# Projecting a query block of one branch ahead of its values, and a shorter stretch of dense work before the first scores

## The chip, the cores and the metric

The kernel runs on one core of one Trainium2 chip. The metric is the device time of one execution in microseconds, as the median of several runs. The engines are named as the profile names them: PE is TensorE's matmuls and PEld its weight loads, DVE is VectorE, ACT is ScalarE, POOL is GpSimd, SP is SyncE, whose queue issues most of the DMAs.

## What is computed

Two layers over one sequence of 1024 tokens of width 1024, float32. Each layer, cut to what matters here:

```python
h = rms_norm(x, g_pre)
p = h @ w_in                      # one projection, split by columns:
(u_a, v_a, gate_a, q_b, k_b, v_b, gate_b, q_c, k_c, v_c, gate_c, merge_logits) = split(p)
y_a = chunk_gmlp(u_a, v_a, ...) * silu(gate_a)
qh, kh = rope(q_b), rope(k_b)     # 8 query heads of 64, 2 key/value heads
y_b = sliding_window_attention(qh, kh, v_b, sinks) * silu(gate_b)   # window 128, softmax with sinks
y_c = stick_breaking_attention(q_c, k_c, v_c) * silu(gate_c)        # 4 heads of 128, causal
gates = sigmoid(merge_logits + b_merge)
merged = gates[0]*(y_a @ w_ba) + gates[1]*(y_b @ w_bb) + gates[2]*(y_c @ w_bc)
x = x + rms_norm(merged @ w_out, g_post)
```

Branch B is the sliding-window attention. The change lies in the order of its projections.

## The kernel before, in words

Every float32 product is made of three matmuls in a rounded format: each operand is split into a high part (a ScalarE cast, L111) and a low part (a VectorE subtraction, L112), and `mm3` (L128 to L130) adds high times high, high times low and low times high. A dense group of the projections is one such triple on 512 columns.

TensorE's instructions stand in the order in which the program issues them. The other engines' orders are set by the Tile scheduler, with its own priorities; they can be read from the built program alone.

The projections of a layer are jobs in one queue, `stream`. A job (`proj_t`) makes 128 output columns for all 1024 tokens: two halves of 512 tokens, each of eight groups accumulated in a PSUM buffer `pj` (two buffers), and an evacuation after each half. `step()` issues one group; `fill(us)` issues groups until a planned time is used up, at 0.64 planned us per group of `proj_t` and 0.32 per group of `proj_n`; `need(label)` issues groups until the named job has ended, and since the end is only noticed when the next step is asked for, it issues the first group of the following job as well. A job loads the weights of the job behind it when it starts.

`queue_layer` sets the jobs' order: values, queries and keys of branch C, then for branch B the first query block `qb(0)`, the keys `kb`, the values `vb`, the other query blocks `qb(1)` to `qb(3)` and the gates, and the values of branch A (`proj_n`). Each `qb(hp)` holds two heads. Its second evacuation (L279) calls `after_q`: `rope` swaps halves of the heads by four DMAs (L292, SP's queue), VectorE multiplies and adds (L293, L294, L295), and for each of two heads ScalarE copies a high part (L346) and VectorE subtracts a low one (L347). `after_k` does alike for the keys (L307, L309). `after_v` sets two deferred steps, 4 and 6 planned us behind `vb`: each transposes half of the values (L323, TensorE) and splits them; the second also makes differences (L330).

`branch_c` goes first and uses up the queue by `fill` between its own matmuls. `branch_b` follows: `need("vb")`, a `fill`, then eight score blocks. `scores(v)` (matmuls L492) needs query block `v // 2`; it uses two `pz` buffers in turn, which ScalarE (L499, L500, L505) and VectorE (L503, L506, a mask) empty, and is followed by a softmax (L510 to L518). scores(0) and scores(1) stand ahead of the loop, scores(v + 2) in its turn v, then `transp` (L526) and `attend` (L550, evacuated by L560 and L561) of block v, with a `fill` between any two.

`dense` comes behind branch B. It first issues what is left of the queue, and then the products of a two-by-two matrix scheme with seven products each. Their weight operands are `wop`; their data operands are the halves of h and the combinations T1, T2, T4 (own tiles) and T3 (written over a part of h once the queue no longer reads it), built on VectorE from blocks of h that are loaded again (L688; L699, L703, L705, L710, then splits). In each scheme the first two products read h, the third T2, the fourth T3. L823 adds products.

## Time and profile before

| what | us |
|---|---|
| median of 3 runs (2031.05 to 2033.9) | 2031.58 |
| the profiled execution | 2034.41 |
| its span, first to last instruction | 2032.7 |
| TensorE busy in the span | 1997.0 |
| VectorE, ScalarE, GpSimd busy | 1250.1, 811.9, 466.5 |

The profile shows one execution. Busy time counts the time in which an engine works on an instruction. An "idle before" with a releaser says how long an engine stood still ahead of an instruction and whose result it took to go on. Two matmuls overlap, the start of one with the end of the one before, so the rate is read from start to start. In the timeline, neighbouring instructions of one kind are merged into a row with a count. Layer 0 takes about the first half of the span, and its branch B starts near 267 us; the same place of layer 1 is near 1270 us.

### The profile page before, as it was taken

Reading aid. Unit: us, or ns where it says so; the run is one execution under the profiler, and the core shown is the slowest. Engines: PE = TensorE matmul, PEld = TensorE weight load, DVE = VectorE, ACT = ScalarE, POOL = GpSimd, SP = SyncE. Lnnn points to the kernel's source line nnn. Section 1 sums busy time; section 2 is a strip of 40 time slices with the busy share of each in tenths; the row PEclk is TensorE's granted clock in tenths of the full one; section 3 lists DMA queues with packets and bytes.
Section 4 is the critical chain, followed back from the end, with each engine's and each line's share of the span. In section 5 each row is a group of like instructions: output and inputs, shape, how many; then the busy total and the mean of one; then the engine's idle time right before and its main releaser. Section 6 shows DMA issues by size and latency. Waiting matters only on the chain.

```text
span 2032.7 us, 26630 instructions
## 1 busy us (share of the span) xinstructions
PE 1997.0 (98%) x10169; PEld 1676.4 (82%) x10169; DVE 1250.1 (62%) x1649; ACT 811.9 (40%) x1485; POOL 466.5 (23%) x489
## 2 busy tenths in 40 slices
PE   7999999999999999999999999999999999999998
PEld 7898878998888888888898988789888888888886
DVE  5465767776767655554545567677866766555533
ACT  6344555532334433213444345554322444332221
POOL 0221301233422220251002222022343322203400
PEclk9999999999999999999999999999999999999999
DMA  7111222233755527732431112233428554376213
GB/s 230 51 39 45 73 73 94 94 104 104 249 198 186 185 93 252 251 116 86 137 125 40 42 53 62 63 104 104 125 99 273 184 194 157 108 269 217 83 52 135
DMA packets 167008, 261.81 MB, mean 129 GB/s; under 512 B 8617, under 2 KB 120289, under 8 KB 166881
## 3 DMA queue, kind: packets, MB, share of 16 engines
q1 hardware_dynamic: 159968, 234.95, 35.7%
q10 hardware_dynamic: 6912, 25.17, 3.0%
q8 instruction: 80, 1.31, 0.3%
q14 instruction: 48, 0.39, 0.1%
HBM read 175.15 MB, written 79.69 MB: 125 GB/s over the span
## 4 chain that ended last, share of the span: by engine, by line
PE 93%; DVE 3%; ACT 2%; issue 1%; DMA 1%; POOL 0%; SPq 0%; DVEq 0%; ACTq 0%; POOLq 0%
PE pj L129 17%; PE pj L128 17%; PE pj L130 16%; PE pz L129 6%; PE pz L128 6%; PE pz L130 6%; PE ptr L128 5%; PE ptr L129 5%; PE ptr L130 5%; PE pav L427 3%; PE pz L492 1%; PE ptr L414 1%; PE pav L550 1%; PE ptr L526 1%; DMA s<-hT 1%
## 5 line engine op out<-in xcount | busy, mean ns | idle before, releaser
L128 PE MATMUL pj<-h,whi 128*128 128x512 f32 x636 | 260.4, 409 | 1.0 <-ACT s L257 0.8
L129 PE MATMUL pj<-h,whi 128*128 128x512 f32 x636 | 252.4, 397 | 0.0
L130 PE MATMUL pj<-h,wlo 128*128 128x512 f32 x636 | 252.0, 396 | 0.0
L111 ACT CAST wop<-s 128x512 fp32r<-128x512 f32 x144 | 88.2, 618 | 172.7 <-PE ptr L130 56.7
L128 PE MATMUL pj<-whi,h 128*128 128x256 f32 x512 | 148.6, 290 | 1.2 <-ACT h L111 1.2
L130 PE MATMUL pj<-whi,h 128*128 128x256 f32 x512 | 144.6, 282 | 1.7 <-DVE h L112 1.7
L112 DVE TENSOR_TENSOR wlo<-wr,whi 128x1024 fp32r<-128x1024 f32 x76 | 103.7, 1366 | 66.0 <-ACT whi L111 65.8
L129 PE MATMUL pj<-wlo,h 128*128 128x256 f32 x512 | 144.1, 281 | 0.0
L130 PEld LDWEIGHTS pj<-h,wlo 128*128 128x128 f32 x636 | 120.0, 189 | 28.7
L128 PEld LDWEIGHTS pj<-h,whi 128*128 128x128 f32 x636 | 120.5, 190 | 24.4 <-ACT s L257 1.7
L129 PEld LDWEIGHTS pj<-h,whi 128*128 128x128 f32 x636 | 120.4, 189 | 20.2
L111 ACT CAST whi<-wr 128x1024 fp32r<-128x1024 f32 x76 | 79.9, 1051 | 136.1 <-PE pj L129 76.9
L948 POOL TENSOR_TENSOR s<-s,s 128x512 f32<-128x512 f32 x56 | 83.1, 1487 | 221.6 <-DVE s L942 200.7
L112 DVE TENSOR_TENSOR wop<-s,wop 128x512 fp32r<-128x512 f32 x144 | 119.3, 833 | 17.4 <-ACT wop L111 17.3
L112 DVE TENSOR_TENSOR wop<-wr,wop 128x512 fp32r<-128x512 f32 x108 | 96.2, 892 | 39.0 <-ACT wop L111 38.9
L397 DVE TENSOR_TENSOR_SCAN s<-s,ones 128x128 f32<-128x128 f32 (+3 forms) x64 | 88.0, 1375 | 49.6 <-POOL s L392 49.4
L111 ACT CAST wop<-wr 128x512 fp32r<-128x512 f32 x108 | 66.2, 618 | 115.4 <-PE ptr L130 30.4
L112 DVE TENSOR_TENSOR s<-ptr,s 128x512 fp32r<-128x512 f32 (+2 forms) x132 | 76.4, 588 | 56.8 <-ACT s L111 56.5
L129 PE MATMUL pj<-h,s 128*128 128x512 f32 x256 | 102.0, 398 | 0.0
L128 PE MATMUL pj<-h,s 128*128 128x512 f32 x256 | 101.1, 395 | 0.0
L130 PE MATMUL pj<-h,s 128*128 128x512 f32 x256 | 100.6, 393 | 0.0
L130 PEld LDWEIGHTS pj<-whi,h 128*128 128x128 f32 x512 | 97.3, 190 | 2.6 <-DVE h L112 2.6
(226 smaller groups left out, 5132.8 us busy)
## 6 DMA issues: line engine op xcount, KB each, us to landing
wr<-in_w_in_dram SPq DMA_DIRECT2D x88, 512.0 KB, 4.1
sg<-s ACTq DMA_DIRECT2D x48, 512.0 KB, 5.2
s<-sg SPq DMA_DIRECT2D x48, 512.0 KB, 5.0
s<-in_w_in_dram SPq DMA_DIRECT2D x36, 512.0 KB, 4.8
s<-in_x_dram SPq DMA_DIRECT2D x16, 512.0 KB, 4.1
hT<-s SPq DMA_DIRECT2D x16, 512.0 KB, 3.2
s<-hT SPq DMA_DIRECT2D x16, 512.0 KB, 3.8
wor<-in_w_out_dram SPq DMA_DIRECT2D x16, 512.0 KB, 3.7
```

What stands on the lines that cost most here:

```text
L111: nc.scalar.copy(hi, raw)
L112: nc.vector.tensor_tensor(lo, raw, hi.bitcast(F32), op=ALU.subtract)
L128: nc.tensor.matmul(acc, lh, rh, start=first, stop=False)
L129: nc.tensor.matmul(acc, lh, rl, start=False, stop=False)
L130: nc.tensor.matmul(acc, ll, rh, start=False, stop=last)
L397: nc.vector.tensor_tensor_scan(t1[:, :kl][:, ::-1], t1[:, :kl][:, ::-1], ones.to_broadcast([P, kl]), 1.0, op0=ALU.mult, op1=ALU.mult)
L414: nc.tensor.transpose(pt[:, b - b0], t2[:, b * P:(b + 1) * P], ident)
L427: nc.tensor.matmul(av, S["v", hd // 2, b // 4][e][:, vs], at4(at, b, f)[:, b % 4], start=ps_ == 0 and b == 0, stop=ps_ == 2 and b == nb - 1)
L492: nc.tensor.matmul(z[:, e * 2 + j], qT[e][:, n * P:(n + 1) * P], kk[i][:, k0:k0 + 256], start=i == 0, stop=i == 1)
L526: nc.tensor.transpose(pt[:, j * P:(j + 1) * P], s[:, (q * 4 + j) * P:(q * 4 + j + 1) * P], ident)
L550: nc.tensor.matmul(av[:, j], w, t.rearrange("p (e j) k -> p e j k", j=2)[:, :, j], start=i == 0, stop=i == len(ops) - 1)
L948: eng.tensor_tensor(acc[dm][:, ts], acc[dm][:, ts], sg[:, ts], op=ALU.add)
```

## The change

Two edits. In the queue, `qb(1)` is put between `kb` and `vb`. In `branch_b`, the first `fill` goes from 8 to 3 planned us.

```diff
         qb(0)
         raw("kb", O_KB, 1.0, after_k)
+        qb(1)
         raw("vb", O_VB, 1.0, after_v)
-        for i in range(1, 4):
-            qb(i)
+        qb(2); qb(3)
...
         need("vb")
-        fill(8)
+        fill(3)
         ready = {0: scores(0)}
         fill(5)
         ready[1] = scores(1)
```

The work is the same. Up to the end of branch C TensorE issues the same number of groups, and `vb`, which had just ended there, is now the job that `need("vb")` still issues whole.

Three places show what the order becomes. The first is VectorE around the two L347 of qb(1), in layer 0. Before, they stand behind the softmax of scores(0) and scores(1) (tiles s_2688 and s_2779) and directly ahead of the mask of scores(2) (L503, s_2869).

```order
L518 TENSOR_TENSOR s_2688<-s_2688,ls 128x1024
L293 TENSOR_TENSOR s_2654<-s_2654,s_2210 128x1024
L294 TENSOR_TENSOR s_2740<-s_2740,s_2211 128x1024
L516 TENSOR_TENSOR ls<-ls,es 128x8
L295 TENSOR_TENSOR s_2654<-s_2654,s_2740 128x1024
L517 RECIPROCAL ls<-ls 128x8
L112 TENSOR_TENSOR wlo<-wr,whi 128x1024
L518 TENSOR_TENSOR s_2779<-s_2779,ls 128x1024
L347 TENSOR_TENSOR s_2748<-s_2654,s_2748 64x1024
L347 TENSOR_TENSOR s_2749<-s_2654,s_2749 64x1024
L503 COPY_PREDICATED s_2869<-mprev,pz 128x2x128
```

In the change, the same engine has them (s_2591 and s_2592) right behind the keys' L309, ahead of the split of the first half of the values (L112 from ptr) and of the mask of scores(0) (L503, s_2721).

```order
L309 TENSOR_TENSOR s_2450<-s_2339,s_2449 64x1024 x2
L112 TENSOR_TENSOR wlo<-wr,whi 128x1024
L293 TENSOR_TENSOR s_2535<-s_2535,s_2210 128x1024
L294 TENSOR_TENSOR s_2583<-s_2583,s_2211 128x1024
L295 TENSOR_TENSOR s_2535<-s_2535,s_2583 128x1024
L347 TENSOR_TENSOR s_2591<-s_2535,s_2591 64x1024
L347 TENSOR_TENSOR s_2592<-s_2535,s_2592 64x1024
L112 TENSOR_TENSOR wlo<-wr,whi 128x1024
L112 TENSOR_TENSOR s_2683<-ptr,s_2683 128x8x64
L503 COPY_PREDICATED s_2721<-mprev,pz 128x2x128
```

The rotation of qb(1) has moved from behind two softmaxes to ahead of the first.

The second place is ScalarE at the end of branch C (L430 is the evacuation of its last attention) in the change: the high copies of qb(1) (L346) stand on either side of the second evacuation of vb (L279 into s_2655), and the value cast (L111 from ptr) and the copies of scores(0) (L499, L500) behind them.

```order
L111 CAST whi<-wr 128x1024
L430 COPY s_2228<-pav 128x256
L279 ACTIVATE s_2655<-pj 128x512
L346 CAST s_2591<-s_2535 64x1024
L279 ACTIVATE s_2655<-pj 128x512
L346 CAST s_2592<-s_2535 64x1024
L111 CAST whi<-wr 128x1024
L111 CAST s_2683<-ptr 128x8x64
L499 COPY s_2721<-pz 128x2x128
```

Before, the value casts follow directly on L430:

```order
L111 CAST whi<-wr 128x1024
L430 COPY s_2228<-pav 128x256
L111 CAST s_2583<-ptr 128x8x64
L326 COPY s_2587<-ptr 128x512
L279 ACTIVATE s_2654<-pj 128x512
```

So the values' evacuation and casts come later against branch C, and the queries' copies are in between.

The third place is VectorE behind the last attention of branch B (its L561 write s_3902 before), where T2 (s_4262), T3 (h_75, in two parts), T4 (s_4269) and the next weight operands are split. Before:

```order
L703 TENSOR_TENSOR s_3927<-s_4257,s_3927 128x1024
L354 COPY s_3893<-pj 128x2x256
L561 TENSOR_TENSOR s_3902<-pav,s_4231 64x256
L705 TENSOR_TENSOR s_4257<-s_4257,s_3929 128x1024
L561 TENSOR_TENSOR s_3902<-pav,s_4231 64x256
L710 TENSOR_TENSOR s_4265<-s_4265,s_4257 128x1024
L112 TENSOR_TENSOR s_4262<-s_4257,s_4261 128x1024
L112 TENSOR_TENSOR h_75<-s_3903,h_74 128x1024
L354 COPY s_4004<-pj 128x2x256
L112 TENSOR_TENSOR wop<-wr,wop 128x512
L112 TENSOR_TENSOR wop<-s_4247,wop 128x512
L112 TENSOR_TENSOR s_4269<-s_4265,s_4268 128x1024
```

In the change (T2 is s_4303, T4 s_4310, and L561 write s_3941):

```order
L561 TENSOR_TENSOR s_3941<-pav,s_4272 64x256
L112 TENSOR_TENSOR wop<-wr,wop 128x512
L354 COPY s_3978<-pj 128x2x256
L112 TENSOR_TENSOR wop<-s_4288,wop 128x512
L705 TENSOR_TENSOR s_4298<-s_4298,s_3968 128x1024
L112 TENSOR_TENSOR h_75<-s_3942,h_74 128x1024
L710 TENSOR_TENSOR s_4306<-s_4306,s_4298 128x1024
L112 TENSOR_TENSOR s_4303<-s_4298,s_4302 128x1024
L823 TENSOR_TENSOR s_4338<-s_4338,pz 128x512
L112 TENSOR_TENSOR s_4310<-s_4306,s_4309 128x1024
L112 TENSOR_TENSOR h_75<-s_3966,h_74 128x1024
```

The first part of T3 and the weight operands have moved ahead, and the second part of T3 now stands behind the addition L823 of the second product. Between the last attention and the first product of `dense`, TensorE has 54 matmuls of the queue before and 15 in the change, in both layers.

## The prediction

> **What bounds the kernel now.** I read the page first: the busy shares and the chain that ended last.

> ```profile
> span 2032.7 us, 26630 instructions
> PE 1997.0 (98%) x10169; PEld 1676.4 (82%) x10169; DVE 1250.1 (62%) x1649; ACT 811.9 (40%) x1485; POOL 466.5 (23%) x489
> PE 93%; DVE 3%; ACT 2%; issue 1%; DMA 1%; POOL 0%; SPq 0%; DVEq 0%; ACTq 0%; POOLq 0%
> ```

> TensorE is busy 98% of the span, and the chain is TensorE for 93%. The diff adds and removes no matmul, so it can only act on the 35.7 us (2032.7 less 1997.0) in which TensorE is not busy, and on matmuls that run slower than they need to. Hence the second view, whom TensorE waited for (us in total, times, longest).

> ```profile
> PE pz L492 <- DVE s L347: 10.1, 4, 4.7
> PE pz L236 <- DVE s L227: 9.2, 2, 8.3
> PE pav L427 <- DVE s L112: 3.0, 2, 1.5
> PE ptr L526 <- DVE s L561: 2.1, 4, 0.9
> ...
> PE pj L128 <- ACT s L257: 0.8, 2, 0.4
> ```

> The largest wait is branch B's scores (L492) waiting for the rotated query copies (L347): 10.1 us in four waits, two in each layer. L236 is the start of the kernel, which the diff does not touch. The third view is TensorE's timeline at that wait, first in layer 0, then the same place in layer 1 (start, duration, in brackets the idle time and its releaser).

> ```profile
> 285.19 2.08 PE L492 MATMUL pz<-s,s 128*128 128x256 f32 x16
> 287.11 0.39 PE L128 MATMUL pj<-h,whi 128*128 128x512 f32 x1
> ...
> 293.87 0.40 PE L130 MATMUL pj<-h,wlo 128*128 128x512 f32 x1
> 298.92 0.77 PE L492 MATMUL pz<-s,s 128*128 128x256 f32 x2 [4.66 <-DVE s L347]
> 300.08 3.36 PE L492 MATMUL pz<-s,s 128*128 128x256 f32 x14 [0.40 <-DVE s L347]
> 303.24 0.63 PE L128 MATMUL pj<-h,whi 128*128 128x512 f32 x1
> ...
> 308.36 0.60 PE L526 MATMUL ptr<-ident,s 128*128 128x128 f32 x4
> ```

> ```profile
> 1288.35 2.08 PE L492 MATMUL pz<-s,s 128*128 128x256 f32 x16
> 1302.07 0.77 PE L492 MATMUL pz<-s,s 128*128 128x256 f32 x2 [4.65 <-DVE s L347]
> 1311.67 0.60 PE L526 MATMUL ptr<-ident,s 128*128 128x128 f32 x4
> ```

> The wait costs more than 5 us a layer, because after it the matmuls are slow: 0.63 us each where they took 0.39. The stretches of time say why (the figure behind POOL is the granted TensorE clock).

> ```profile
> 299.00:303.00 4.00, 3.60 (x15) 3.31 (x16) 1.47 (x2) 0.65 (x2) 0.41 (x1) 0.50 0.52 146
> 305.40:312.00 6.60, 6.60 (x34) 5.41 (x33) 6.25 (x8) 2.60 (x4) 1.27 (x2) 1.00 0.01 1
> ```

> The clock is at 0.50 behind the gap, and at 1.00 from 305.4 on.

> **The stall, sized without a theory of the clock.** Between 287.11 and 293.87 stand 29 matmul starts after the first, so a 128x512 matmul takes 0.233 us and a dense group of three 0.70 us. Sixteen score matmuls take 287.11 - 285.19 = 1.92 us. From the start of scores(1) to the first transpose (L526) the program has scores(1), ten groups, scores(2) and six groups: 1.92 + 6.99 + 1.92 + 4.20 = 15.03 us. Measured: 308.36 - 285.19 = 23.17 in layer 0 and 1311.67 - 1288.35 = 23.32 in layer 1. The stall costs 8.14 and 8.29 us, together 16.4 us; about 5.2 us of each is idle time, 2.9 us the half clock.

> [...]

> **Why the second projection was late, and where it goes.** Before, qb(1) stands behind vb. Its last evacuation, and VectorE's rotation, are these rows (ScalarE first).

> ```profile
> 295.02 0.59 ACT L279 ACTIVATE s<-pj 128x512 f32<-128x512 f32 x1
> ```

> ```profile
> 291.57 1.22 DVE L293 TENSOR_TENSOR s<-s,s 128x1024 f32<-128x1024 f32 x1
> ...
> 296.31 1.22 DVE L518 TENSOR_TENSOR s<-s,ls 128x1024 f32<-128x1024 f32 x1
> 297.56 2.47 DVE L347 TENSOR_TENSOR s<-s,s 64x1024 fp32r<-64x1024 f32 x2
> ```

> The first score block of qb(1), scores(2), stands right there on TensorE; L347 stands behind the softmax of scores(0) and scores(1). In the change qb(1) takes vb's place, which ended just before the last attention of branch C. What surrounded that place:

> ```profile
> 265.27 0.60 ACT L279 ACTIVATE s<-pj 128x512 f32<-128x512 f32 x1
> ```

> ```profile
> 264.52 3.71 DVE L309 TENSOR_TENSOR s<-s,s 64x1024 fp32r<-64x1024 f32 x3
> ...
> 268.26 1.23 DVE L112 TENSOR_TENSOR wlo<-wr,whi 128x1024 fp32r<-128x1024 f32 x1
> ```

> ```profile
> 247.53 2.75 SPq L292 DMA_DIRECT2D s<-s  x4
> ```

> ```profile
> 267.01 0.39 PE L128 MATMUL pj<-h,whi 128*128 128x512 f32 x1
> ```

> So qb(1) is evacuated at 265.9. Its four swap DMAs (moved with it past two weight loads and branch C's output on SP's queue) take 2.75 us to issue and, allowing as much again to land, are in at 271.4. VectorE is free at 269.5, so L293 to L295 run 271.4 to 275.1 (1.22 each). The first ScalarE copy, taken as long as the L347 it feeds (2.47 / 2), and that L347 end by 277.6. The second copy stands on ScalarE behind vb's second evacuation. vb is 16 groups from 267.01, so that evacuation ends at 278.2 + 0.6; copy and L347 follow until 281.3.

> When does TensorE want it? After 267.01 come 16 groups of vb, one of qb(2) that starting the next job adds, and fill(3), which is five: 22 groups, 15.4 us. Then a transpose block (0.4: the 0.60 of L526's row, four such transposes, less the 0.16 by which a matmul's end overlaps the next), scores(0) 1.92, eight groups 5.6, another 0.4, scores(1) 1.92, ten groups 7.0: scores(2) at 299.6. The copy is there 18 us before. The wait of 10.1 us goes, and with it the half clock.

> The dense work itself is neither lost nor won: eight groups that stood later now stand ahead of scores(2).

> **What is late next, branch B's start.** VectorE now has the rotation ahead of the split of the value transposes and of the mask of scores(0). After L347 at 281.3 come a weight split (1.22) and the value split, which waits for its transpose, done at 282.8. scores(0) ends at 284.7; a ScalarE copy (0.6 as in L279's row) and a mask (1.22 at most, as VectorE's other rows) make 286.5. The next user of the buffers is scores(1), at 290.7: 4.2 us of room. Where qb(2) and qb(3) are wanted (scores(4) and scores(6)), they are projected eight groups earlier than before. Cost here: nothing, hidden behind the 22 + 8 dense groups. If that cover were gone, a late mask would hold scores(1).

> **What is late next, branch B's end.** The eight groups are missing where branch B hands over to the dense products. Before, 54 matmuls of 128x256 stand between the last attention and the first product; in the change 15. The same rows give both lengths (54 matmuls from 431.44 to 437.74, 15 of them until 433.19).

> ```profile
> 431.44 0.28 PE L128 MATMUL pj<-whi,h 128*128 128x256 f32 x1
> ...
> 433.19 0.28 PE L128 MATMUL pj<-whi,h 128*128 128x256 f32 x1
> ...
> 437.74 0.39 PE L128 MATMUL ptr<-h,wop 128*128 128x512 f32 x1
> ...
> 446.13 0.40 PE L128 MATMUL ptr<-h,wop 128*128 128x512 f32 x1
> ```

> ```profile
> 431.76 1.23 DVE L703 TENSOR_TENSOR s<-s,s 128x1024 f32<-128x1024 f32 x1 [1.79 <-DMA s<-hT]
> ...
> 435.19 0.43 DVE L561 TENSOR_TENSOR s<-pav,s 64x256 f32<-64x256 f32 x1
> 436.32 1.23 DVE L710 TENSOR_TENSOR s<-s,s 128x1024 f32<-128x1024 f32 x1 [0.70 <-DMA s<-hT]
> ...
> 440.45 0.68 DVE L112 TENSOR_TENSOR wop<-wr,wop 128x512 fp32r<-128x512 f32 x1
> ...
> 442.79 1.22 DVE L112 TENSOR_TENSOR h<-s,h 128x1024 fp32r<-128x1024 f32 x1
> ```

> The products come 437.74 - 433.19 = 4.55 us sooner after the last attention, while VectorE's work still starts at 431.76, when a DMA lands. The fourth product (446.13) needs T3, whose last split ended at 442.79 + 1.22 = 444.0: 2.1 us of room, now 4.55 wanted. On the clock of the last attention, the order in the change puts L703, two L561, two wop splits, L354, L705, the first T3 split, L710, the T2 split, one L823, the T4 split and the second T3 split: seven operations of 128x1024 (1.22), two L561 (0.43) and four of 128x512 (0.68), 12.1 us, so T3 is done between 443.0 (starts overlap ends by 0.08) and 443.9. The fourth product starts at 446.13 - 4.55 = 441.6 and reads the second half's split after seven matmuls, 1.6 us, at 443.2. Wait: 0 to 0.7 us a layer by this sum, 2.4 if nothing were reordered and the whole product had to wait. I take 0.25, near the first, because the order shows the reordering; both layers 0.5 us.

> Small waits on L526 and L257 (2.1 + 0.8 us) can go or double when the phase moves: -2.9 to +2.9, taken as zero.

> **The sum.** -16.4 + 0.5 = -15.9 us. The profiled execution, 2034.4 us for a span of 2032.7, would go to 2018.5; it stood 2.8 us above the median shown, so the median goes from 2031.6 to 2015.7.

> **Rivals.** *The gain is given back at the end of branch B.* Against it: the sum above. For it: a room of 0.2 us in 12. At its price of 2.4 us a layer the gain is 16.4 - 4.8 = 11.6, time 2020.0. Whether such a gap also slows the clock is open; a gap of 1.48 us in branch C did not:

> ```profile
> 252.55 2.42 PE L427 MATMUL pav<-s,s 128*128 128x256 f32 x18 [1.48 <-DVE s L112]
> 254.80 0.39 PE L128 MATMUL pj<-h,whi 128*128 128x512 f32 x1
> ```

> With 4.55 us and another 2.9 us of half clock a layer, the gain would be 16.4 - 14.9 = 1.5 us, time 2030.1. [...]

> *Slower: the mask of scores(0) behind the rotation.* VectorE takes its work in the order written, so if the swap DMAs came so late that L347 ended more than 4.2 us behind my time, scores(1) would wait for the masks. A layer's gain of 8.2 us is used up when that wait reaches 5.3 us and brings 2.9 us of half clock with it, that is with L347's end at 281.3 + 4.2 + 5.3 = 290.8. At 293 the loss is 2.3 us a layer and the time 2036.2. Against it: swaps issued at 265.9 would have to land past 280, and they are issued in 2.75 us.

> *The change does not do what it says*: L347 still later than 299.6, time 2031.6. It would need 18 us of delay.

> **Chances.** Forecast (gain 13.5 to 19.3): 0.80. End of branch B takes 3 to 12 us: 0.12. Nothing left, by its worst form or because the wait stays: 0.04. Slower by the mask: 0.04. About 0.2% (4.1 us) is what a measurement can tell from no change, so faster 0.92, same 0.04, slower 0.04. The range: low 2031.6 - 16.4 - 2.9 = 2012.3; high 2022.0, the first rival at its face price with 2 us on top.

> **What would show it.** No wait of L492 on L347 in either layer; score matmuls of scores(2) at 0.28 us; a granted clock of 1.00 there; L526's first block 2.7 us earlier (near 305.7 in layer 0), and the first dense product 8 us earlier. The second L347 of qb(1) ends near 281. If a wait of a product on a T3 or T2 split stands within 12 us of the first product, the first rival is at work, and its length says how much of the gain it takes. I am wrong if TensorE's total idle time falls by less than 8 us.

## The result, and the profile after

| | before | after |
|---|---|---|
| median of the runs, us | 2032.3 (4 runs, 2031.05 to 2033.9) | 2017.11 (4 runs, 2016.88 to 2017.93) |
| ratio after to before | | 0.9923 (95% interval 0.991 to 0.9937) |
| profiled execution and its span, us | 2034.41, 2032.7 | 2017.0, 2015.3 |

The change makes the kernel 15.2 us faster; the prediction was a gain of 15.9 us and a time of 2015.7. The page of the kernel after shows the busy shares and, in the third line, the chain that ended last.

```profile
span 2015.3 us, 26620 instructions
PE 1990.3 (99%) x10169; PEld 1670.7 (83%) x10169; DVE 1245.7 (62%) x1649; ACT 809.6 (40%) x1485; POOL 468.0 (23%) x489
PE 93%; DVE 3%; ACT 1%; DMA 1%; issue 1%; POOL 1%; SPq 0%; DVEq 0%; ACTq 0%; POOLq 0%
```

TensorE issues the same 10169 matmuls and is busy 6.7 us less: mostly the matmuls that ran at half clock (about 2.9 us a layer). The rest of the 17.4 us of span, 10.7 us, is idle time. Whom TensorE waits for now (us in total, times, longest):

```profile
PE pz L236 <- DVE s L227: 9.1, 2, 8.2
PE pav L427 <- DVE s L112: 3.0, 2, 1.5
PE ptr L526 <- DVE s L561: 2.0, 4, 0.7
...
PE ptr L129 <- DVE h L112: 0.2, 1, 0.2
PE pj L129 <- DVE h L112: 0.2, 1, 0.2
```

No wait of L492 on L347 is left, nor the 0.8 us of L257. The last two rows are new, and they are the fourth dense product of each layer waiting for T3. TensorE's timeline at scores(1), scores(2) and the first transpose of branch B, layer 0 and then layer 1:

```profile
289.44 2.07 PE L492 MATMUL pz<-s,s 128*128 128x256 f32 x16
298.34 2.08 PE L492 MATMUL pz<-s,s 128*128 128x256 f32 x16
304.44 0.60 PE L526 MATMUL ptr<-ident,s 128*128 128x128 f32 x4
```

```profile
1284.80 2.07 PE L492 MATMUL pz<-s,s 128*128 128x256 f32 x16
1293.69 2.08 PE L492 MATMUL pz<-s,s 128*128 128x256 f32 x16
1299.80 0.38 PE L526 MATMUL ptr<-ident,s 128*128 128x128 f32 x2
```

All sixteen matmuls of scores(2) run without a gap. From scores(1) to L526 it is 15.00 us in both layers, where before took 23.17 and 23.32. The stretch of time there (engines in the order PE, PEld, DVE, ACT, POOL; then the granted clock) shows a full clock:

```profile
290.00:300.00 10.00, 10.00 (x57) 8.64 (x56) 7.21 (x12) 7.51 (x25) 0.00 (x0) 1.00 0.24 55
```

VectorE has the second query block ready long before, and the masks of scores(0) are not held up by it (L506 is the second of them):

```profile
273.67 1.22 DVE L347 TENSOR_TENSOR s<-s,s 64x1024 fp32r<-64x1024 f32 x1 [1.16 <-ACT s L346]
278.76 1.22 DVE L347 TENSOR_TENSOR s<-s,s 64x1024 fp32r<-64x1024 f32 x1 [3.88 <-ACT s L346]
284.31 0.74 DVE L506 COPY_PREDICATED s<-mprev,pz 128x512 f32<-128x512 int32 x1 [0.53 <-ACT s L505]
```

The end of branch B is where a part of it is lost again. TensorE's last attention, the first dense product, and the places in the third and the fourth product that start late:

```profile
424.97 1.11 PE L550 MATMUL pav<-s,s 128*128 128x256 f32 x8
...
427.68 0.40 PE L128 MATMUL ptr<-h,wop 128*128 128x512 f32 x1
...
435.19 0.51 PE L129 MATMUL pj<-s,wop 128*128 128x512 f32 x1
...
438.49 0.50 PE L129 MATMUL ptr<-h,wop 128*128 128x512 f32 x1 [0.25 <-DVE h L112]
```

Positions in a layer are best counted from the last attention of branch C (the last L427), because the whole kernel starts up to 1.8 us earlier or later in one of these traces than in another: that row is at 264.14 before and at 262.81 after, and between 262.33 and 264.14 in all of them. Up to it TensorE runs matmuls of the same number and shape in both kernels, and the difference is there from about the fiftieth matmul on, long ahead of anything that was moved. The table gives, for each layer (0 / 1), the starts of the last attention of branch B (L550), of the first dense product and of the first L632 counted so, read from the timelines, and how far the last two lie apart. From the first L632 of layer 0 to the last L427 of layer 1 it is 801.6 us before and after.

| kernel (FB: the fill FB[0] explained below) | median, us | last L550 | first product | L632 | product to L632 |
|---|---|---|---|---|---|
| before | 2032.3 | 166.35 / 166.79 | 173.60 / 174.04 | 201.59 / 202.02 | 27.99 / 27.98 |
| after | 2017.11 | 162.16 / 162.16 | 164.87 / 164.87 | 193.78 / 193.77 | 28.91 / 28.90 |
| before, FB 11 | 2017.07 | 162.30 / 162.42 | 165.01 / 165.13 | 193.22 / 193.90 | 28.21 / 28.77 |
| before, FB 7 | 2033.54 | 167.17 / 167.13 | 174.08 / 174.03 | 202.04 / 202.00 | 27.96 / 27.97 |
| before, FB 8 | 2034.26 | 168.79 / 168.68 | 174.29 / 174.19 | 202.26 / 202.15 | 27.97 / 27.96 |
| after, FB 3 | 2029.05 | 165.80 / 165.57 | 171.31 / 171.08 | 199.27 / 199.04 | 27.96 / 27.96 |
| after, FB 3, another slot | 2024.62 | 163.61 / 163.82 | 169.12 / 169.33 | 197.08 / 197.29 | 27.96 / 27.96 |
| after, FB 5, block 7 fill 1.0 less | 2016.29 | 160.43 / 160.45 | 165.24 / 165.25 | 193.20 / 193.22 | 27.96 / 27.97 |
| after, block 7 fill 1.0 less | 2014.93 | 161.08 / 161.08 | 164.83 / 164.83 | 193.05 / 192.78 | 28.22 / 27.95 |
| after, block 7 fill 1.6 less | 2015.34 | 160.19 / 160.27 | 164.64 / 164.73 | 192.63 / 192.71 | 27.99 / 27.98 |

The two layers lose 7.81 and 8.25 us between before and after, 16.1 of the 17.4; 1.33 us are the start of that execution. The profiled execution of before (2034.41) is slower than its median, so the medians differ by less, 15.2 us; what the other 0.9 us are made of no trace here shows.

### The profile page after: what moved, and what is told of

The parts are those of the page before. It is cut to its first block, busy times and chain, and to the rows that moved or that the text cites. A ratio compares the mean times of both kernels' runs of the same rounds, so it can differ in the third digit from the quotient of the medians.

```text
span 2015.3 us, 26620 instructions
## 1 busy us (share of the span) xinstructions
PE 1990.3 (99%) x10169; PEld 1670.7 (83%) x10169; DVE 1245.7 (62%) x1649; ACT 809.6 (40%) x1485; POOL 468.0 (23%) x489
## 4 chain that ended last, share of the span: by engine, by line
PE 93%; DVE 3%; ACT 1%; DMA 1%; issue 1%; POOL 1%; SPq 0%; DVEq 0%; ACTq 0%; POOLq 0%
PE pj L129 17%; PE pj L130 17%; PE pj L128 17%; PE pz L129 6%; PE pz L130 6%; PE pz L128 6%; PE ptr L129 5%; PE ptr L130 5%; PE ptr L128 5%; PE pav L427 3%; PE pz L492 2%; PE ptr L414 1%; PE pav L550 1%; DMA s<-hT 1%; DVE s L112 1%
## 5 line engine op out<-in xcount | busy, mean ns | idle before, releaser
L128 PE MATMUL pj<-h,whi 128*128 128x512 f32 x636 | 259.0, 407 | 0.1
L130 PE MATMUL pj<-h,wlo 128*128 128x512 f32 x636 | 251.4, 395 | 0.0
L111 ACT CAST wop<-s 128x512 fp32r<-128x512 f32 x144 | 87.2, 618 | 159.0 <-PE ptr L130 48.1
L128 PE MATMUL pj<-whi,h 128*128 128x256 f32 x512 | 148.6, 290 | 0.9 <-ACT h L111 0.9
L130 PE MATMUL pj<-whi,h 128*128 128x256 f32 x512 | 144.5, 282 | 1.7 <-DVE h L112 1.7
L112 DVE TENSOR_TENSOR wlo<-wr,whi 128x1024 fp32r<-128x1024 f32 x76 | 102.9, 1356 | 66.0 <-ACT whi L111 65.5
L130 PEld LDWEIGHTS pj<-h,wlo 128*128 128x128 f32 x636 | 119.5, 188 | 28.5
L128 PEld LDWEIGHTS pj<-h,whi 128*128 128x128 f32 x636 | 119.8, 188 | 22.9 <-ACT s L279 1.0
L111 ACT CAST whi<-wr 128x1024 fp32r<-128x1024 f32 x76 | 80.0, 1053 | 134.8 <-PE pj L129 77.7
L112 DVE TENSOR_TENSOR wop<-s,wop 128x512 fp32r<-128x512 f32 x144 | 118.5, 829 | 14.7 <-ACT wop L111 14.5
L112 DVE TENSOR_TENSOR wop<-wr,wop 128x512 fp32r<-128x512 f32 x108 | 97.0, 899 | 34.9 <-ACT wop L111 34.5
L111 ACT CAST wop<-wr 128x512 fp32r<-128x512 f32 x108 | 65.8, 617 | 113.2 <-POOL wr L758 32.1
L112 DVE TENSOR_TENSOR s<-ptr,s 128x512 fp32r<-128x512 f32 (+2 forms) x132 | 76.7, 588 | 50.2 <-ACT s L111 49.9
L128 PE MATMUL pj<-h,s 128*128 128x512 f32 x256 | 101.1, 395 | 0.0
L130 PE MATMUL pj<-h,s 128*128 128x512 f32 x256 | 100.6, 393 | 0.0
L130 PEld LDWEIGHTS pj<-whi,h 128*128 128x128 f32 x512 | 97.2, 190 | 2.6 <-DVE h L112 2.6
```

The lines of the kernel that those rows point to most:

```text
L111: nc.scalar.copy(hi, raw)
L112: nc.vector.tensor_tensor(lo, raw, hi.bitcast(F32), op=ALU.subtract)
L128: nc.tensor.matmul(acc, lh, rh, start=first, stop=False)
L130: nc.tensor.matmul(acc, ll, rh, start=False, stop=last)
```

## The experiments

Two theories went into them. The first, from the prediction: the whole gain is the wait of scores(2) with the half clock behind it, so what counts is how late the queries are against the dense work ahead of scores(2), and the dense work missing at the end of branch B costs the 0.9 us per layer of the table's last column. The rival: each edit alone brings something of its own, the reorder or the shorter fill. FB[0] is the fill between scores(1) and scores(2); before and after have 6 there. (Three of the recorded expectations place it wrongly, between scores(0) and scores(1) or ahead of scores(1); each edit shows what was changed.)

**The reorder alone.** The change with the first fill left at 8:

```diff
         need("vb")
-        fill(3)
+        fill(8)
```

> The new order of the projections with the first fill left at 8. TensorE then has another eight groups (5.6 us) ahead of scores(0), and the queue runs empty inside branch B: the last fills of the eighth block issue nothing. My theory, that the dense work is only a cover and has to last to the end of branch B, expects no wait of the scores on L347, and new waits of TensorE on the last transposes and attentions, some 3 to 6 us a layer, with more waits in the first products: 2022 to 2030 us. The rival, that the moved projection alone makes the gain and the shorter fill is idle, expects the changed kernel's time, 2017, within 1 us.

Measured: 2030.68 us (10 runs), ratio to before 0.9988 (0.9979 to 0.9997). The wait on L347 is gone, and eight groups more are used up early, so that the queue runs dry inside branch B. Its waits of TensorE from 385 to 445 us, and the stretch at the end of the branch:

```profile
PE pav L550 <- POOL s L533: 3.1, 2, 1.6
PE ptr L128 <- DVE s L561: 2.8, 1, 2.8
PE ptr L526 <- DVE s L561: 1.6, 1, 1.6
```

```profile
425.00:435.00 10.00, 4.18 (x26) 3.50 (x25) 6.11 (x10) 3.77 (x9) 6.62 (x6) 0.84 0.36 118
```

TensorE is busy 4.18 of 10 us there, and the clock goes down again. The gain at scores(2) is given back nearly whole, 0.7 us beyond the upper end of what was expected.

**The shorter fill alone.** Before, with 3 instead of 8 as the first fill:

```diff
         need("vb")
-        fill(8)
+        fill(3)
```

> The first fill at 3, with the projections in the old order. scores(2) is then wanted eight groups (5.6 us) earlier, while qb(1) is projected at the same time as before. My theory, that the stall is the distance between qb(1)'s evacuation and scores(2), expects the wait on L347 to grow from 5 to 7 to 10 us a layer, half clock behind it as before, and a time 4 to 11 us above the kernel before, 2036 to 2043. The rival, that less dense work ahead of the scores is itself a gain, expects 2025 to 2031.

Measured: 2047.26 us (4 runs), ratio 1.007 (1.0057 to 1.0084). Whom TensorE waited for, and the row of scores(2):

```profile
PE pz L492 <- DVE s L347: 22.4, 4, 10.8
```

```profile
298.95 0.77 PE L492 MATMUL pz<-s,s 128*128 128x256 f32 x2 [10.79 <-DVE s L347]
```

scores(2) starts at 298.95, where before had 298.92: VectorE's time sets it, and the work taken away ahead of it only lengthens the wait, by 6.1 us a layer. That is 12.3 us of waiting and, by the medians, 14.6 us of time. The direction is the theory's and the wait near the 7 to 10 us that it gave; its range of times ended 4 us lower.

**No reorder, dense work ahead of scores(2) instead.** Before, with the fill between scores(1) and scores(2) at 11:

```diff
-FB = (6, 1.4, 1.4, 1.7, 2.2, 2.2)
+FB = (11, 1.4, 1.4, 1.7, 2.2, 2.2)
```

> The old order and the old first fill, but the fill between scores(1) and scores(2) at 11 instead of 6: eight more groups (5.6 us) stand ahead of scores(2), as many as in the changed kernel, and 15 matmuls are left behind branch B, as there. My theory, that only the amount of dense work between the projection and scores(2) matters, expects the wait on L347 to shrink from 5 us to 0 to 0.6 us a layer, no half clock, and the changed kernel's time: 2017 to 2019. The rival, that the place of qb(1) on VectorE ahead of the softmax is what made the gain, expects the rotation to stay as late as it was relative to scores(2), a wait of 2 us or more a layer, and 2022 or more.

Measured: 2017.07 us (5 runs), ratio 0.9923 (0.9909 to 0.9936): the change's own time and inside the theory's range, with the queue in the old order. No wait on L347, no half clock, and 15 matmuls left behind the last attention, as in the change. The row of scores(2), all sixteen without a gap:

```profile
298.15 2.32 PE L492 MATMUL pz<-s,s 128*128 128x256 f32 x16
```

So the reorder brought nothing that the longer fill does not bring; it is one of two ways to have scores(2) stand behind the queries.

**Half way.** The same edit with 8 (shown) and with 7, which puts 13 and 11 groups there instead of 10:

```diff
-FB = (6, 1.4, 1.4, 1.7, 2.2, 2.2)
+FB = (8, 1.4, 1.4, 1.7, 2.2, 2.2)
```

> The kernel before with its first fill between scores(0) and scores(1) unchanged in place but two planned us longer (8 instead of 6), order of the queue as before: 13 groups instead of 10 stand between scores(1) and scores(2), so the matrix unit reaches scores(2) about 3 x 1.92 = 5.8 us later while the queries are ready at the same time; 39 matmuls less are left for the end of branch B. Theory (the half clock behind a wait comes from the length of the wait, and 1.48 us did not bring it): the wait at scores(2) falls from 4.7 to about 2.7 us in a first matmul and nothing runs at half clock behind it; the saving against before is 2 us of wait + 2.9 us of half clock + the second wait, less 0.2 for the smaller rest, so 4 to 5 us per layer: 2022 to 2024. Rival (any wait of over 2 us brings the half clock): saving only the 2 us per layer: 2027 to 2029.

> As the other, with one planned us more (7 instead of 6): 11 groups between scores(1) and scores(2), the wait falls to about 4.1 us. Theory: a wait of 4.1 us is still close to the 4.66 us that brought the half clock; with the half clock behind it 2030 to 2031, without it 2024 to 2026. The run tells on which side of the bound it lies. Rival (each group of dense work takes 1.92 us off the wait and no more): 2027.5.

Measured: 2034.26 us (10 runs), ratio 1.0007 (0.9998 to 1.0016) with 8, and 2033.54 us (10 runs), 1.0005 (0.9996 to 1.0014) with 7. Both expectations missed, those of the theory and of the rival: nothing is gained. (They also speak of 1.92 us for a dense group; it is 0.70, and 1.92 is sixteen score matmuls. And with 8 it is 39 matmuls that are left at the end, not 39 fewer. The waits forecast, 2.7 and 4.1 us, go with 0.70, and came out at 2.6 and 4.0.) Two rows of TensorE's timeline with 8, and one of ScalarE's, show where it went:

```profile
297.60 0.47 PE L492 MATMUL pz<-s,s 128*128 128x256 f32 x2 [2.55 <-DVE s L347]
```

```profile
329.58 0.52 PE L128 MATMUL pj<-h,whi 128*128 128x512 f32 x1 [2.21 <-ACT s L257]
```

```profile
328.94 0.59 ACT L257 COPY s<-pj 128x512 f32<-128x512 f32 x1 [0.67 <-DVE s L347]
```

The first wait is shorter by the 2.1 us of three groups, as it should be. The second is longer than anything that L257 cost before (0.4 us): a product group waits for a PSUM buffer that L257, a gate's evacuation, has still to empty, and L257 itself had waited for the last query block's L347, of which more below. Over both layers the scores' waits on L347 fall from 10.1 to 6.5 us and those on L257 rise from 0.8 to 4.4: one has taken the other's place. And both bring the half clock, though 2.55 and 2.21 us are about half of what before waited. With 7, 0.7 us of the first wait are saved and others come, among them this one, 1.4 us in each layer:

```profile
PE pj L129 <- DVE wlo L112: 2.8, 2, 1.4
```

So at 7 and 8 the time did not fall by the dense work put in, because other waits came up, and at 11, where none of these waits is left, it fell whole; 9 and 10 were not run.

**More cover at the end of the branch, from ahead of scores(2).** The change with FB[0] at 3:

```diff
-FB = (6, 1.4, 1.4, 1.7, 2.2, 2.2)
+FB = (3, 1.4, 1.4, 1.7, 2.2, 2.2)
```

> The changed kernel with the fill between scores(1) and scores(2) at 3 instead of 6: five groups fewer there, so that 39 matmuls instead of 15 are left between branch B's last attention and the first product. My theory, that the 0.9 us a layer lost in the first products comes from the short cover, expects these waits to be gone, still no wait on L347, and 1.5 to 2.0 us less than the changed kernel: 2015.1 to 2015.6. The rival, that the loss comes from the other order on VectorE or other buffers and not from the cover, expects 2017.

Measured: 2029.05 us (11 runs), ratio 0.9984 (0.9976 to 0.9993). The loss at the end of the branch is gone (27.96 us from the first product to L632), and yet the expectation was missed by some 13.5 us. TensorE now waits for L257 once in each layer, 9.4 us together. The place on TensorE, ScalarE and VectorE:

```profile
327.34 0.68 PE L128 MATMUL pj<-h,whi 128*128 128x512 f32 x1 [4.71 <-ACT s L257]
```

```profile
326.70 0.59 ACT L257 COPY s<-pj 128x512 f32<-128x512 f32 x1 [0.38 <-DVE s L347]
```

```profile
325.45 1.22 DVE L347 TENSOR_TENSOR s<-s,s 64x1024 fp32r<-64x1024 f32 x1
```

The first gate's evacuation (L257) waits for the second L347 of the last query block, as it did with 8 above. The two have no data in common. Tiles are given out from a list of free slots, and in this build the gate's tile gets the slot of that block's raw query tile, whose last reader is L347; in the change it got that of the block's swap tile, whose last reader is L295. The kernel before with FB[0] at 8 deals the raw tile's slot too, with 7 it does not.

**Is it the slot?** The same, with the first gate's tile taken from the second free slot:

```diff
-                    ev.g = new()
+                    keep = free.popleft() if br == "b" and c == 0 else None
+                    ev.g = new()
+                    if keep is not None:
+                        free.appendleft(keep)
```

> The change with its first fill between scores(0) and scores(1) at 3, as in the run that missed (2029.05), and one edit more: the first gate's tile is taken from the second free slot instead of the first, so that it no longer inherits the slot of the last query block's raw tile; nothing else moves but the place of that copy on ScalarE. Theory (the 4.7 us wait at the gate comes from the slot alone): the wait of L128 on L257 is gone, no half clock there, the stretch from branch C's last attention to L632 falls from 199.2 to 192.7-193.3 us per layer: 2015.2 to 2016.8. Rival (ScalarE or the two product buffers are simply behind in that stretch, whatever the slot): the wait stays at 2 us or more, 2022 to 2029.

Measured: 2024.62 us (5 runs), ratio 0.9961 (0.9949 to 0.9974). Between theory and rival: the wait on L257 is gone, and 4.4 us are won, but a wait of 3.04 us stands close behind it, now at a transpose that needs an attention's evacuation. (The edit adds three lines, so the lines of this kernel are three higher: L529 is L526, L564 is L561, L350 is L347.) TensorE, then VectorE:

```profile
326.84 0.63 PE L529 MATMUL ptr<-ident,s 128*128 128x128 f32 x4 [3.04 <-DVE s L564]
```

```profile
323.85 0.42 DVE L564 TENSOR_TENSOR s<-pav,s 64x256 f32<-64x256 f32 x1
324.30 1.22 DVE L350 TENSOR_TENSOR s<-s,s 64x1024 fp32r<-64x1024 f32 x1
325.55 0.69 DVE L256 COPY s<-pj 128x512 f32<-128x512 f32 x1
326.27 0.43 DVE L564 TENSOR_TENSOR s<-pav,s 64x256 f32<-64x256 f32 x1
```

VectorE works almost without a gap here, 22.59 of the 23 us from 305 to 328 (22.19 in the run before this one). So the slot alone is not the whole of the loss; it chose which of VectorE's results TensorE met first. What stands behind it is argued and not tested: five groups fewer ahead of scores(2) bring TensorE to all that follows 3.5 us earlier, while VectorE's work there is no shorter.

**More cover from a fill of the last block.** The change, with one fill of the last score block (block 7) shortened by 1.0, and by 1.6 planned us, so that 24 and 30 matmuls of the queue are left behind the last attention instead of 15. FB_MORE is added to the fill between a block's two transposes, so this is not the last fill of the branch, as the expectations call it; two attentions come behind it:

```diff
-FB_MORE = {1: 2.3, 2: 1.3}
+FB_MORE = {1: 2.3, 2: 1.3, 7: -1.0}
```

> The change, with one planned us less in the last fill of branch B (before the last attention): 24 matmuls of the queue instead of 15 are left behind the last attention. Theory (the change lost 0.9 us per layer at the end of branch B because the first two products came before their T2 and T3): three more groups of cover, no other place touched, win back 0.3 to 0.7 us per layer, 2015.7 to 2016.6. Rival (the loss there is not from the cover but from slower work of VectorE there): no change, 2017.1.

> The change, with 1.6 planned us less (instead of 1.0) in the last block's fill: 33 matmuls or so of the queue are left behind the last attention instead of 24 (2014.93) and 15 (the change, 2017.11). Theory (24 matmuls cover T2 and T3 but for 0.2 us in layer 0; more cover has nothing left to win): 2014.5 to 2015.2, with 27.95 us from the first product to L632 in both layers. Rival (the dense work taken from ahead of the last attention is missed there, and the attention waits for its transposes' copies): 2015.5 to 2018, with a wait of L550 in the last block.

Measured: 2014.93 us (5 runs, 2014.74 to 2015.12), ratio to before 0.9914 (0.99 to 0.9927), with 1.0; 2015.34 us (5 runs, 2014.51 to 2015.82), 0.9914 (0.9901 to 0.9928), with 1.6. The first is outside the range of the change's runs (2016.88 to 2017.93), and 0.8 us better than its expectation; the second is 0.1 us above the theory's range, with no wait of L550. The first product comes at the same time as in the change (164.83 against 164.87), but the last attention 1.08 us earlier, and VectorE's first step for the products (L703) 0.74 us. VectorE with 1.0 less:

```profile
425.34 1.22 DVE L703 TENSOR_TENSOR s<-s,s 128x1024 f32<-128x1024 f32 x1 [2.33 <-DMA s<-hT]
...
430.56 1.22 DVE L112 TENSOR_TENSOR s<-s,s 128x1024 fp32r<-128x1024 f32 x1
...
433.28 2.35 DVE L112 TENSOR_TENSOR h<-s,h 128x1024 fp32r<-128x1024 f32 x2
```

T2 and T3 are split by 431.8 and 435.6, and no matmul of the third and the fourth product starts late; the 0.25 us left in layer 0 are in the fifth. VectorE's order is another here too: both splits of T3 stand ahead of T4's, where the change has the second one behind it. So these runs do not tell the longer cover from the better order that came with it. With 1.6 nothing more is won that the runs could tell: the last column of the table is at its floor.

**Both.** The change with FB[0] at 5 and the fill of block 7 shorter by 1.0 (33 matmuls left):

```diff
-FB = (6, 1.4, 1.4, 1.7, 2.2, 2.2)
-FB_MORE = {1: 2.3, 2: 1.3}
+FB = (5, 1.4, 1.4, 1.7, 2.2, 2.2)
+FB_MORE = {1: 2.3, 2: 1.3, 7: -1.0}
```

> The change, with one planned us less ahead of scores(1) (5 instead of 6) and one less in the last fill: 33 matmuls are left behind the last attention, 8 groups between scores(1) and scores(2). The evacuation of the gate that waited 4.7 us for its buffer in the run with 3 takes a buffer here which is free behind the third query block's L295, as in the change. Theory: no wait at the gate, the loss at the end of branch B is gone as in the run with 3 (0.9 us per layer), 2015.2 to 2015.8. Rival (less dense work ahead of scores(2) itself brings the wait at the gate): 2020 to 2029, with a wait of over 2 us at the gate's first groups.

Measured: 2016.29 us (4 runs, 2015.24 to 2016.54), ratio 0.9919 (0.9906 to 0.9933). No wait at the gate, and the end of the branch is at its floor, but 0.7 us a layer goes to a weight split that is late, and the time is 0.5 us above the theory's range. The lowest median of all these runs is that of the change with block 7's fill 1.0 shorter. Its traces are 0.73 and 0.99 us a layer shorter than the change's up to L632, but the 95% intervals of the two ratios to before overlap (0.9900 to 0.9927 against 0.9910 to 0.9937).

## Why the prediction was right, and where not

- **The stall.** Predicted: 16.4 us, from 15.03 us of work against 23.17 and 23.32. Measured: 15.00 in both layers, so 16.5 us. The half clock went with the wait, as said. That the sum was made without a theory of the clock is what made it good: with one stretch of 3.41 us at half clock in each layer, as the last section shows it with FB[0] at 8, it would have been an estimated 13.8 (5.2 us of idle time and 1.7 of half clock a layer), and before had two such stretches in a row.
- **Its steps.** The second L347 of qb(1) was to end at 281.3 on the clock of before; it ended at 279.98 on a clock 1.33 us earlier. scores(2) was to start at 299.6, and started at 298.34, the same. The masks of scores(0) were due by 286.5, and the second and last of them was done at 285.05. L526 came at 304.44, predicted 305.7. With the 1.33 us added all of these are met to 0.2 us.
- **One row was read wrongly.** The ScalarE row at 295.02, given as qb(1)'s last evacuation, is qb(2)'s. qb(1)'s stands 13 us earlier, in before's timeline of ScalarE:

```profile
281.92 0.59 ACT L279 ACTIVATE s<-pj 128x512 f32<-128x512 f32 x1
```

The last of its swaps was issued at 284.4 and they landed 2.3 us after their issue, so they were in by 286.7, and VectorE took them up at 291.57, behind the masks and a reduction of scores(1) and the softmax of scores(0). Almost 5 us of the lateness were thus VectorE's queue, as much as the first wait of scores(2); what the order of projection had in it no run separates. The sum did not use the row; the account of the cause did.
- **The end of branch B** is the term that was mis-sized: 0.25 us a layer, between 0 and 0.7, and measured 0.92 (28.91 against 27.99 from the first product to L632). What failed is that the sum counted T3's wait alone. The third product waits for T2 too: its row at 435.19 above starts 0.30 us late and the next matmul 0.11. The fourth, waiting for T3, loses 0.42 and 0.10, which alone lies inside the range. And the sum took 1.22 us for each operation of 128x1024, while T3's last split took longer. The row of VectorE, and then two of GpSimd, in the kernel after:

```profile
436.78 1.65 DVE L112 TENSOR_TENSOR h<-s,h 128x1024 fp32r<-128x1024 f32 x1
```

```profile
435.97 1.39 POOL L615 TENSOR_SCALAR_AFFINE_SELECT s<-s 128x512 f32<-128x512 f32 x1 [10.15 <-DMA s<-in_gm_w_s_dram]
437.44 2.14 POOL L755 TENSOR_TENSOR s<-s 128x512 f32<-128x512 f32 x1
```

T3's split took 1.65 us beside GpSimd's operations, 0.43 longer than in the kernel before (1.22), about what the fourth product waited (0.42). Before, GpSimd's L755 came at 444.58, when T3 was done.
- **The rivals.** The gain given back at the end of the branch was at work, with 0.9 us a layer of its 2.4, and without the half clock. The other two did not show.
- **The small waits**, taken as zero between -2.9 and +2.9, gave -1.4 us up to the first product: 17.9 us were won there, 16.5 of them the stall. Of this 0.8 is L257's wait; 0.6 I cannot place. They made up for the mis-sized term (1.84 us for both layers instead of 0.5). That the two cancel, and the total comes so near, is luck; that the stall's own size was met is not.

## What to carry to other kernels

When one engine waits because another is late, count what stands between them on both: dense work put ahead of the waiting instruction did the same here as the work done earlier, and it had to be enough for the whole wait, since 0.7 and 2.1 us of it brought nothing, other waits coming up in place of the first. Dense work moved forward is missing somewhere, so look for the place where the engine now arrives first, and count its other queues there with the durations they have beside each other (T3's split took 1.65 us here and 1.22 in before). A tile that takes its slot from a list of free ones can inherit a wait on a reader it has nothing to do with, as the first gate's did with FB[0] at 3, and a change of order deals these anew.

## What the runs showed of the hardware

In these traces the half clock does not follow the length of a wait. In one execution of the kernel with the other slot the same wait of 3.04 us stands in both layers; behind it the transposes take 0.63 us in layer 0 (the row above) and 1.09 in layer 1:

```profile
1325.51 1.09 PE L529 MATMUL ptr<-ident,s 128*128 128x128 f32 x4 [3.04 <-DVE s L564]
```

```profile
295.02:298.43 3.41, 0.00 (x0) 0.00 (x0) 3.38 (x5) 2.56 (x4) 0.00 (x0) 1.00 0.43 100
298.43:301.84 3.41, 2.52 (x10) 2.26 (x11) 1.57 (x2) 0.07 (x1) 0.00 (x0) 0.50 0.77 207
301.84:305.26 3.42, 3.42 (x13) 3.03 (x13) 1.61 (x3) 1.16 (x3) 0.41 (x1) 0.50 0.00 1
```

FB[0] at 8:

```profile
326.52:329.93 3.41, 1.20 (x6) 0.67 (x5) 3.32 (x4) 2.32 (x3) 0.00 (x0) 1.00 0.00 0
329.93:333.34 3.41, 3.41 (x12) 2.72 (x11) 2.75 (x4) 0.59 (x1) 0.74 (x2) 0.50 0.43 159
```

The other slot, layer 0 and layer 1:

```profile
325.01:328.42 3.41, 1.58 (x9) 1.43 (x10) 3.29 (x5) 1.95 (x4) 0.20 (x1) 1.00 0.37 154
...
1321.71:1325.12 3.41, 0.76 (x4) 0.29 (x2) 3.29 (x5) 3.01 (x4) 0.00 (x0) 1.00 0.10 37
1325.12:1328.54 3.42, 3.03 (x10) 2.58 (x11) 3.33 (x5) 1.07 (x2) 1.19 (x2) 0.50 0.37 153
```

One stretch each of the reorder alone, of before in layer 1, and of the change with FB[0] at 3 in layer 1:

```profile
1428.40:1431.82 3.42, 1.42 (x10) 1.01 (x8) 0.73 (x2) 0.00 (x0) 3.34 (x4) 1.00 0.41 134
```

```profile
1301.95:1305.37 3.42, 2.91 (x12) 2.65 (x13) 1.22 (x1) 0.46 (x2) 0.01 (x1) 0.50 0.67 184
```

```profile
1327.60:1331.01 3.41, 2.82 (x9) 2.33 (x10) 3.28 (x5) 0.82 (x2) 0.00 (x0) 0.50 0.27 43
```

Of these stretches, those at full clock with 1.42 us of work or less were followed by half clock, the one with 1.58 not. The way back is less clear: stretches at half clock with 2.52 and 2.91 us of work were followed by another, those with 2.82 and 3.03 not, so TensorE's busy time as the profile counts it does not decide it alone. That before paid 2.9 us of half clock is two stretches of 3.41 in each layer. The first of the two still held a part of the long wait and the short one of 0.40; that these kept it low is likely and not shown. That a stretch need not be wholly idle is shown here by the 1.20 and 1.42 us. Where the limits lie was not tried.

The second is VectorE beside GpSimd: 1.65 us instead of 1.22 for one subtraction of 128x1024, and 2.14 instead of 1.29 for GpSimd's L755 at the same time (1.29 in the kernel with FB[0] at 3, where it ran at 442.45 beside VectorE's weight splits). No run took GpSimd's work away, so that the one made the other longer is the author's reading and not shown. Nor is it always VectorE that is longer: in the change its L295 at 306.34 took 1.22 us beside two of GpSimd's L533, which together took 2.32 us instead of 1.22 (before, at 427.50, where VectorE stood idle).
